# A hybrid decoder step on one core: what the first stage loads and computes, and the order around the output projection

## The chip, the cores and the metric

One Trainium2 chip, one core. The metric is the device time of one execution in microseconds. One core has TensorE (PE in the profile, its weight loads PEld), VectorE (DVE), ScalarE (ACT), GpSimd (POOL) and SyncE (SP). SP and ACT each issue transfers on a DMA queue of their own (SPq, ACTq).

## The reference, cut to what matters

A prompt of 512 tokens and 8 sample tokens (520 rows of 1024) pass one layer: adaLN modulation, RMSNorm, an input projection, sparse attention and a gated recurrence, an output projection, and a mixture of experts. What the change touches:

```python
sh_a, sc_a, gt_a, sh_f, sc_f, gt_f = split(silu(c) @ w_ada + b_ada, 6)
h = rms_norm(x, g_pre_mix) * (1.0 + sc_a) + sh_a
q, kv_c, kv_s, kv_w, gates, hq, hf, hi, hog = split_projection(h @ w_in)
kvc = compress_kv(concat([pool_c[page_table], kv_c]), w_phi1, b_phi1, w_phi2)   # samples: 8 x 1024 cached rows
mixed = concat([rms_norm(o_nsa), o_hgrn]) @ w_out
x = x + gt_a * rms_norm(mixed)
```

`compress_kv` turns each chunk of cached rows into one row by two small matmuls with a gelu between them. The modulation weights `w_ada` are 1024 x 6144, in three parts of 1024 x 2048 (8.4 MB each): part 0 (shift and scale before the mixer) is needed before the input projection, parts 1 and 2 only after the output projection.

## The kernel before, in words

The program is written with generators. `play(order, ...)` advances one generator per letter of a string, which sets the program order. A planner then places each engine's instructions by that order and its own estimate of when inputs are ready and buffers free, so an instruction can come ahead of earlier ones on its engine. `issue_after(i)` holds what a block creates on the engine of instruction `i` behind `i`.

Stage A, played by `ORD_A` (line 56, played at line 373), has three generators:

- `x`, `normed(t)` (line 348), five times: a tile of 128 rows of x is loaded on ACT's queue, squared and summed, scaled, and transposed on TensorE into `xnT`.
- `a`, `ada(0)` (line 218): for each of 8 values of k two tiles of 128 x 1024 of `w_ada` (512 KB each) are loaded on SP's queue into the buffers `mh0` to `mh3` and `wa`, and multiplied with `sT`. At the end the bias and gain table `bg` (512 KB) goes into the next of the same buffers (line 235), and VectorE makes `mod0` (lines 237, 240).
- `s`, `sample_compress` (line 296): the 8 samples' cached pages are loaded in 8 batches `cg` of 8 pages (128 KB a page, 1 MB a batch, three batches buffered), first stage 32 matmuls (line 311, into PSUM bank `pf` or `po` in turn), evacuated and passed through the gelu on ScalarE and VectorE (lines 318 to 322, 275 to 279), second stage 8 matmuls (lines 326 and 329). One batch is two letters.

After stage A: the first projection's weights `wr0` (512 KB) are loaded into buffer `mh1` and split in a high and a low part (lines 374 to 377, helper lines 114 and 115), `mod0` is transposed (line 380), and `hhi`, `hlo` (the modulated rows in two parts) are made (lines 382 to 393).

Stage B, played by `ORD_B` (line 539): ten projections of 48 matmuls and a narrow one for the gates (`n`, lines 410 and 474), the rest of `samples`, and parts 1 and 2 of the modulation (`a`) with 1 MB loads into two buffers, whose memory is free only when `hlo` is done. The result goes to DRAM (`MOD`). Parts 1 and 2 accumulate in `pf`. The stages that follow (recurrence, attention) are bound by the same engine.

Output projection: the last attention block `attn(3)` (`d`, line 1060) has eight steps of scores (lines 1071, 1073), exponentials (line 1077) and values (line 1085). `ORD_E` (line 60, played at line 1230) plays it with the splits of the first half of `w_out` (`f`, line 1211: `ewh` and its low part) and of `mixT` (`mhh`). `wout` (line 1294) is the projection, `wout_samples` (line 1307) the one for the samples, `router_weights` (line 1363) transposes a table of the modulation for the router.

Of the kernel before, what the change touches and what calls it, by code (L numbers as in the profile page):

```python
# [11 lines left out]
F32 = mybir.dt.float32  # L12
# [38 lines left out]
NWA = 1  # L51
FIRST = 6
# [3 lines left out]
ORD_A = "xaxsaaxaxssssaaaxsassaaas"  # L56
ORD_B = "ssnaasnaanaanaanaasnaanaansnaannsnassnasaa"
# [9 lines left out]
def body(tc, I, O):  # L67
# [45 lines left out]
    def split(src, hi, lo, eng=None):  # L113
        act.activation(hi, src, AF.Copy)  # L114
        (eng or dve).tensor_tensor(lo, src, hi.bitcast(F32), op=ALU.subtract)  # L115

# [101 lines left out]
    def ada(gq, tiles, ps_1, mod):  # L218
        p = ps_1()
        for k in range(KT):  # L220
            if gq:
                w2 = tiles()
                sp.dma_start(w2, I["wa"][gq, k].rearrange("j p n -> p j n"))
            for j in range(2):
                if gq:
                    wa = w2[:, j]
                else:
                    wa = tiles()
                    sp.dma_start(wa, I["wa"][gq, k, j])
                for q in range(2):  # L230
                    r = slice(64 * j + 32 * q, 64 * j + 32 * q + 32)
                    pe.matmul(p[r, :], sT[:, k, :], wa[:, 512 * q:512 * q + 512], start=(k == 0), stop=(k == KT - 1))
            yield
        bg = (tiles()[:, 0] if gq else tiles()).rearrange("p (a b) -> p a b", a=2)
        sp.dma_start(bg, I["bg"][gq])
# [52 lines left out]
    sp.dma_start(w1c, I["wphi"])  # L288
    w2c = pc_.tile([64, 2, 64], F32, name="w2c")
    sp.dma_start(w2c, I["wphi2"])  # L290
    b1c = pc_.tile([64, 2], F32, name="b1c")
    sp.dma_start(b1c, I["b1"])
# [3 lines left out]
    def sample_compress():  # L296
        cgs = []
# [6 lines left out]
        for b in range(8):  # L304
# [3 lines left out]
            p = (ps_f if b % 2 and b < FIRST else ps_o)()  # L308
# [57 lines left out]
    def all_normed():  # L366
        for t in range(5):
            normed(t)
            yield

    was = itertools.cycle([lambda c=c: mslot[c](F32, D) for c in range(4)] + [lambda: p0.tile([128, D], F32, name="wa", bufs=1)] * NWA)
    samples = sample_compress()
    play(ORD_A, x=all_normed(), a=ada(0, lambda: next(was)(), lambda: ps_mm()[:, 0], mod0), s=steps(samples, ORD_A.count("s")))
    wr0 = mslot[1](F32, KT, 128)
    act.dma_start(wr0, I["wi"][0])
    wi0 = [mslot[c](F32R, KT, 128) for c in (2, 3)]
    split(wr0, *wi0)
# [157 lines left out]
    def modulations():  # L535
        for gq in (1, 2):
            yield from ada(gq, lambda: wap.tile([128, 2, D], F32, name="wa", bufs=2), ps_f, None)
# [650 lines left out]
    with contextlib.ExitStack() as order:  # L1188
# [21 lines left out]

        def wout_half(hf, wh, wl):
# [18 lines left out]
        play(ORD_E, h=hs, d=gens["d"], f=fh)  # L1230
# [62 lines left out]

    def wout(hf, t, wh, wl):
        pm = ps_mm()
        for kk in (2, 3, 0, 1):
            for k2 in range(2):
                k = 2 * (kk % 2) + k2
                a, b = (mhi[k], mlo[k]) if kk < 2 else (mhh[k], mlh[k])
                for j, (a, b) in enumerate(((a, wh), (a, wl), (b, wh))):  # L1300
                    pe.matmul(pm[:, kk // 2], a[:, 128 * t:128 * t + 128], b[kk][:, k2],
                              start=(k == 0 and j == 0), stop=(k == 3 and j == 2))
        m = x1[t][:, 512 * hf:512 * hf + 512]
# [59 lines left out]
    def router_weights():  # L1363
        dve.tensor_tensor(cW[:, 0], router(GC.rearrange("p a b -> p (a b)"), 128, wrt), brt, op=ALU.add)
# [690 lines left out]
```

## Time and profile before

| | us |
|---|---|
| median of 3 runs | 747.39 (746.75 to 752.22) |
| profiled execution | 741.32 |
| its span | 739.6 |
| mean granted clock of TensorE | 0.958 of full |

The span is the part of the profiled execution in which engines work; 1.7 us lie around it. "Idle before" in a row is the time its engine stood still ahead of it and, after the arrow, what ended that. In a window's row the numbers are busy microseconds, with the count of instructions in brackets.

### The profile page before, as it was taken

To read this page: it belongs to the slowest core of one execution; us is meant where nothing else is said; L and a number is where in the kernel's file an instruction comes from. 1 tells how busy PE (TensorE), PEld (TensorE's weight loads), DVE (VectorE), ACT (ScalarE), POOL (GpSimd) and SP (SyncE) were. 2 spreads that over 40 slices of the span, in tenths; PEclk is the share of its full clock that TensorE was granted. 3 is DMA by queue.
4 is the path that set the end of the run, shared out by engine and by line. 5 is a ranking of instruction groups with operands and counts; after the bars stand their busy time and mean duration, and the time that the engine had idled before them with its cause. 6 is when DMAs were issued, how large, how long until landed. Compare 5 with 4: busy or idle time off the path is not lost. (4 is left out here: it accounts for less than half of the span.)

```text
span 739.6 us, 13131 instructions
## 1 busy us (share of the span) xinstructions
PE 643.4 (87%) x4510; PEld 480.1 (65%) x4510; DVE 456.3 (62%) x1092; ACT 372.2 (50%) x770; POOL 153.4 (21%) x183
## 2 busy tenths in 40 slices
PE   3886898999899989899999989995889999999940
PEld 1754766779688778799776546573456677666620
DVE  3722623345686875667885254456887966888824
ACT  3322523324554545462554545346475757888833
POOL 1000310001141050150110131634211222222113
PEclk9998999999999999999999999998799999999985
DMA  8887698875554545312632274349899889998526
GB/s 282 278 292 252 219 322 294 309 260 176 184 181 143 174 125 182 118 58 85 265 119 84 92 250 140 120 136 345 279 384 356 260 230 321 346 331 287 156 31 231
DMA packets 74605, 160.83 MB, mean 217 GB/s; under 512 B 11346, under 2 KB 39538, under 8 KB 74146
## 3 DMA queue, kind: packets, MB, share of 16 engines
q1 hardware_dynamic: 59808, 125.98, 49.7%
q10 hardware_dynamic: 10690, 25.39, 10.1%
q0 software_dynamic: 4032, 8.53, 5.3%
q8 instruction: 38, 0.62, 0.4%
q14 instruction: 37, 0.30, 0.1%
HBM read 145.29 MB, written 24.28 MB: 229 GB/s over the span
## 5 line engine op out<-in xcount | busy, mean ns | idle before, releaser
L576 PE MATMUL pp<-hhi,wh 128*128 128x260 f32 x256 | 74.9, 292 | 0.3 <-ACT kvt L454 0.3
L576 PE MATMUL pp<-hlo,wh 128*128 128x260 f32 x256 | 73.1, 286 | 0.0
L576 PE MATMUL pp<-hhi,wl 128*128 128x260 f32 x256 | 72.9, 285 | 0.0
L1720 POOL DMA_INDIRECT Y<-ot,gi x17 | 24.4, 1438 | 129.9 <-ACT ot L1719 122.8
L668 ACT ACTIVATE jn<-P,M 128x128 bf16<-128x128 f32 (+3 forms) x64 | 35.9, 561 | 29.2 <-DVE M L666 24.0
L576 PEld LDWEIGHTS pp<-hhi,wh 128*128 128x128 f32 x256 | 48.2, 188 | 3.1 <-issue 2.4
L576 PEld LDWEIGHTS pp<-hlo,wh 128*128 128x128 f32 x256 | 48.2, 188 | 2.0 <-issue 1.8
L576 PEld LDWEIGHTS pp<-hhi,wl 128*128 128x128 f32 x256 | 48.2, 188 | 1.4 <-issue 1.2
L115 DVE TENSOR_TENSOR wl<-wr,wh 128x1024 fp32r<-128x1024 f32 x9 | 11.3, 1250 | 38.4 <-ACT wh L114 38.4
L1077 ACT ACTIVATE PT<-mm 128x256 f32<-128x256 f32 x80 | 24.3, 389 | 19.8 <-PE mm L1073 19.8
L666 DVE CUSTOM_DVE_ANT_0 P<-mm,tb 128x128 f32<-128x128 f32 (+3 forms) x64 | 29.1, 484 | 5.8 <-PE mm L659 5.8
L410 PE MATMUL mm<-hhi,wh 128*128 128x260 f32 x144 | 30.0, 288 | 1.3 <-ACT wh L114 1.3
L114 ACT ACTIVATE wh<-wr 128x1024 fp32r<-128x1024 f32 x9 | 9.5, 1056 | 41.7 <-PE mm L410 22.1
L410 PE MATMUL mm<-hlo,wh 128*128 128x260 f32 x144 | 30.0, 285 | 0.0
L659 PE MATMUL mm<-ka,qs 128*128 128x512 f32 (+2 forms) x112 | 27.3, 352 | 3.1 <-DVE mx L779 1.7
L1691 PE MATMUL pf<-ewi,xh 128*96 128x512 f32 x72 | 29.8, 413 | 0.0
L410 PE MATMUL mm<-hhi,wl 128*128 128x260 f32 x144 | 29.8, 287 | 0.0
L1691 PE MATMUL pf<-ewi,xl 128*96 128x512 f32 x72 | 28.8, 400 | 0.0
L1718 ACT ACTIVATE ot<-mm 96x512 f32<-96x512 f32 x17 | 10.1, 594 | 33.3 <-PE mm L1715 33.3
L1073 PE MATMUL mm<-qs,ka 128*128 128x512 f32 x80 | 25.6, 399 | 0.0
L410 PEld LDWEIGHTS mm<-hhi,wh 128*128 128x128 f32 x144 | 22.2, 188 | 5.0 <-issue 3.4
L410 PEld LDWEIGHTS mm<-hhi,wl 128*128 128x128 f32 x144 | 22.2, 188 | 3.5 <-issue 3.4
(657 smaller groups left out, 1838.6 us busy)
## 6 DMA issues: line engine op xcount, KB each, us to landing
ewr<-in_ew SPq DMA_DIRECT2D x37, 512.0 KB
wa<-in_wa SPq DMA_DIRECT2D x16, 1024.0 KB
wr<-in_wi ACTq DMA_DIRECT2D x25, 512.0 KB
ewt<-in_ew SPq DMA_DIRECT2D x24, 512.0 KB
cg<-in_cc SPq DMA_DIRECT2D x64, 128.0 KB
ewh<-in_ew SPq DMA_DIRECT2D x16, 512.0 KB
x<-in_ew SPq DMA_DIRECT2D x15, 512.0 KB
mh<-in_wa SPq DMA_DIRECT2D x13, 512.0 KB
```

The source lines that it names most:

```text
L114: act.activation(hi, src, AF.Copy)
L115: (eng or dve).tensor_tensor(lo, src, hi.bitcast(F32), op=ALU.subtract)
L410: pe.matmul(p[:, hf, 0:260], a[:, k, :], b[:, k, hf * 260:hf * 260 + 260], start=(k == 0 and j == 0), stop=(k == KT - 1 and j == 2))
L576: pe.matmul(p[:, 0:260], a[:, k, :], b[:, k, c], start=(k == 0 and j == 0), stop=(k == KT - 1 and j == 2))
L659: pe.matmul(o, QS[g][:, h % 4, qc], KA[g][:, j, a:b], start=(j == 0), stop=(j == 1))
L666: dve.tensor_tensor_reduce(out=p, in0=sb[:, br], in1=tb0[:, 384 - 128 * i:512].rearrange("p (k n) -> p k n", n=128), scale=SL[h], scalar=1 ...
L668: act.activation(jn[:, 0:128 * (i + 1)], p.rearrange("p k n -> p (k n)"), AF.Exp, scale=-1.0, bias=M[:, 0, i, br, h:h + 1], accum_out=M[:, ...
L1073: pe.matmul(S[:, br], KS[g][:, q, br, j], QS[g][:, :, qc], start=False, stop=(q == 1))
L1077: act.activation(PT[:, :, h], S4[:, :, h], AF.Exp, scale=-SL[4 * g + h])
L1691: pe.matmul(pg, a[:, k, :], b[:, wk_], start=(k == 0 and j == 0), stop=(k == 7 and j == 2))
L1718: act.activation(o3[:, 0], pd[:, 0], AF.Copy)
L1720: pool.indirect_dma_start(out=Y, out_offset=bass.IndirectOffsetOnAxis(ap=gix, axis=0), in_=ot, in_offset=None, bounds_check=T - 1, oob_is_ ...
```

## The change

- Stage A plays only `x` and `a` (`ORD_A`). The `w_ada` tiles are now 1 MB (both halves of one k), in four buffers: two tiles in the memory of `AK` and `AG`, two in that of `qs0` and `qs1`. `bg` has a tile of its own, loaded on ACT's queue after the last x tile, as is `wr0`, which is also split there.
- The loads of `w_phi1`, `w_phi2`, `b_phi1` and all of `sample_compress` belong to stage B (`ORD_B`), every batch in PSUM bank `po`.
- Parts 1 and 2 of the modulation use four 1 MB buffers: `AK`, `AG` and the two of before.
- `split` returns its ScalarE instruction. In `ORD_E` the steps of `attn(3)` after the first are held on ScalarE behind the second split of `w_out` (one step) or the fourth (the others). The first transposes of `router_weights` are held on TensorE behind the first `wout`.

```diff
-ORD_A = "xaxsaaxaxssssaaaxsassaaas"
-ORD_B = "ssnaasnaanaanaanaasnaanaansnaannsnassnasaa"
+ORD_A = "xaxaxaxaxaaaa"
+ORD_B = "nsasnasansasnasansasnasansasnasansasnasansanaa"
...
     def split(src, hi, lo, eng=None):
-        act.activation(hi, src, AF.Copy)
+        cut = act.activation(hi, src, AF.Copy).ins
         (eng or dve).tensor_tensor(lo, src, hi.bitcast(F32), op=ALU.subtract)
+        return cut
...
+            w2 = tiles()
+            sp.dma_start(w2, I["wa"][gq, k].rearrange("j p n -> p j n"))
             for j in range(2):
-                if gq:
-                    wa = w2[:, j]
-                else:
-                    wa = tiles()
-                    sp.dma_start(wa, I["wa"][gq, k, j])
+                wa = w2[:, j]
...
     def sample_compress():
+        sp.dma_start(w1c, I["wphi"])
+        sp.dma_start(w2c, I["wphi2"])
+        sp.dma_start(b1c, I["b1"])
...
-            p = (ps_f if b % 2 and b < FIRST else ps_o)()
+            p = ps_o()
...
-        for t in range(5):
+        for t in range(4):
             normed(t)
             yield
+        normed(4)
+        act.dma_start(wr0, I["wi"][0])
+        act.dma_start(bg0, I["bg"][0])
+        split(wr0, *wi0)
+        yield
...
+    two = [lambda n=n: wide(at1.tile([128, 2 * D], F32, name=n)) for n in ("AK", "AG")]
+    was = itertools.cycle(two + [lambda n=n: wide(nso.tile([128, 2 * D], F32, name=n)) for n in ("qs0", "qs1")])
...
+        was = itertools.cycle(two + [lambda: wap.tile([128, 2, D], F32, name="wa", bufs=2)] * 2)
         for gq in (1, 2):
-            yield from ada(gq, lambda: wap.tile([128, 2, D], F32, name="wa", bufs=2), ps_f, None)
+            yield from ada(gq, lambda: next(was)(), ps_f, None)
...
-                split(raw[c], high[c], lo, en(93 + c))
+                cuts.append(split(raw[c], high[c], lo, en(93 + c)))
...
-        play(ORD_E, h=hs, d=gens["d"], f=fh)
+        last = dict(h=hs, d=gens["d"], f=fh)
+        for n, c in enumerate(ORD_E):
+            with tc.issue_after(cuts[1 if n < 6 else 3]) if cuts and c == "d" else nullcontext():
+                next(last[c], None)
+        play("", **last)
...
+        wout_end.append(mm.ins)
...
-        dve.tensor_tensor(cW[:, 0], router(GC.rearrange("p a b -> p (a b)"), 128, wrt), brt, op=ALU.add)
+        with tc.issue_after(wout_end[0]):
+            dve.tensor_tensor(cW[:, 0], router(GC.rearrange("p a b -> p (a b)"), 128, wrt), brt, op=ALU.add)
```

## Rows read from the trace of the kernel before

**Rows 1.** Part 1 of the page: busy time, share, instructions.

```profile
PE 643.4 (87%) x4510; PEld 480.1 (65%) x4510; DVE 456.3 (62%) x1092; ACT 372.2 (50%) x770; POOL 153.4 (21%) x183
```

**Rows 2.** Windows: busy by engine, granted clock, DMA share, GB/s.

```profile
core 0: us, PE busy (x) PEld busy (x) DVE busy (x) ACT busy (x) POOL busy (x), PEclk, DMA share, GB/s
0.00:76.17 76.17, 51.45 (x342) 36.07 (x342) 30.18 (x112) 23.53 (x55) 2.82 (x20) 0.93 0.81 269
64.00:70.00 6.00, 2.79 (x15) 2.53 (x16) 1.38 (x2) 0.00 (x0) 0.00 (x0) 0.76 0.90 291
76.17:183.00 106.83, 99.38 (x806) 79.65 (x806) 45.08 (x81) 36.43 (x66) 13.43 (x19) 1.00 0.79 269
0.00:5.00 5.00, 0.00 (x0) 0.00 (x0) 0.00 (x0) 1.59 (x2) 2.23 (x15) 1.00 0.55 182
5.00:10.00 5.00, 0.00 (x0) 0.00 (x0) 0.00 (x0) 0.40 (x2) 0.00 (x0) 1.00 1.00 370
35.00:40.00 5.00, 3.90 (x32) 2.62 (x30) 0.70 (x2) 0.91 (x3) 0.00 (x0) 1.00 0.93 337
```

**Rows 3.** Lines of TensorE, 0 to 76.17 us.

```profile
L311 PE MATMUL po<-cg,w1c 128*128 128x128 f32 x98 | 14.6, 305 | 0.8 <-DMA cg<-in_cc 0.8
L311 PE MATMUL pf<-cg,w1c 128*128 128x128 f32 x96 | 14.0, 307 | 2.7 <-DMA cg<-in_cc 2.7
```

**Rows 4.** Timeline of the SP queue: start us, us, line, transfer.

```profile
63.53 0.38 SPq L235 DMA_DIRECT2D mh<-in_bg  x1
...
79.27 0.33 SPq L215 DMA_DIRECT2D mh<-in_csk  x1
```

**Rows 5.** Timeline of TensorE: start us, us, line [idle before].

```profile
62.72 1.05 PE L232 MATMUL mm<-mh,sT 128*32 128x512 f32 x4 [1.56 <-DMA mh<-in_wa]
...
76.17 0.51 PE L410 MATMUL mm<-hhi,mh 128*128 128x260 f32 x2 [0.87 <-ACT mh L114]
...
90.73 0.33 PE L326 MATMUL pt<-hidc,w2c 64*64 64x64 f32 x4
```

**Rows 6.** Timeline of VectorE and ScalarE, 57 to 73 us.

```profile
57.48 0.27 ACT L318 ACTIVATE Bsc<-po 64x128 f32<-64x128 f32 x1 [2.51 <-PE po L311]
...
60.89 0.42 DVE L279 SCALAR_TENSOR_TENSOR hidc<-huc,hidc 64x256 f32<-64x256 f32 x1 [0.48 <-ACT huc L278]
...
68.43 0.69 DVE L237 TENSOR_TENSOR mod<-mm,mh 128x512 f32<-128x512 f32 x1 [7.12 <-DMA mh<-in_bg]
...
72.00 0.80 ACT L391 ACTIVATE hhi<-xnT,modT 128x512 fp32r<-128x512 f32 x1
```

**Rows 7.** Timeline of TensorE, one whole batch of compression.

```profile
172.94 3.73 PE L311 MATMUL po<-cg,w1c 128*128 128x128 f32 x32
176.43 0.49 PE L410 MATMUL mm<-hhi,wh 128*128 128x260 f32 x2
```

**Rows 8.** Waits of TensorE, 76 to 168 us: total, times, longest.

```profile
PE pf L232 <- DMA wa<-in_wa: 5.1, 8, 1.5
```

**Rows 9.** Timeline of ScalarE before the output projection.

```profile
424.30 3.89 ACT L114 ACTIVATE ewh<-wq 128x1024 fp32r<-128x1024 f32 x4
428.09 1.66 ACT L114 ACTIVATE mhh<-mixT 128x512 fp32r<-128x512 f32 x3
429.65 2.01 ACT L1077 ACTIVATE PT<-mm 128x256 f32<-128x256 f32 x7
```

**Rows 10.** Timeline of TensorE at the same place.

```profile
426.02 0.63 PE L1073 MATMUL mm<-qs,ka 128*128 128x512 f32 x2
429.11 1.92 PE L1314 MATMUL pf<-ewr,msn 128*32 128x512 f32 x2 [2.46 <-DVE ewr L115]
...
432.55 0.65 PE L1085 MATMUL po<-PT,VT 128*64 128x256 f32 x4
```

**Rows 11.** Waits of ScalarE, 395 to 470 us.

```profile
ACT PT L1077 <- PE mm L1073: 13.5, 8, 3.3
```

**Rows 12.** Timeline of TensorE, the router's first transposes.

```profile
444.70 1.09 PE L1347 MATMUL pt<-ident,tab 128*128 128x128 f32 x8
```

More of the change, by code (lines that the diff above doesn't have):

```diff
@@ L3 @@
 import contextlib
-from contextlib import ExitStack
+from contextlib import ExitStack, nullcontext
 import numpy as np
@@ L50 @@
 LOP = ()
-NWA = 1
-FIRST = 6
 DMAN = False
 NCG = 3
-ORD_A = "xaxsaaxaxssssaaaxsassaaas"
-ORD_B = "ssnaasnaanaanaanaasnaanaansnaannsnassnasaa"
+ORD_A = "xaxaxaxaxaaaa"
+ORD_B = "nsasnasansasnasansasnasansasnasansasnasansanaa"
 ORD_C = "PPPrPsPrPPrPsPrPPsPrPPrPsPrPPrsPPPrPsPrPPrttsPPrPPrsPPPrsPPrPPrsPPrPsPPrPPrsPPrttPsPrPPrPsPPrPsPrPPrPsPrPPsPrPPrPsPrttPPrsPPrPPsPrPPrsPPrPPrsPPPrsPPPPsPPPsPPPPPPPPPtt"
@@ L215, in paged, with ada @@
                 sp.dma_start(t[:, p], I[src][bass.ds(rs[p], 1)].rearrange("o p f -> p (o f)"))
-    def ada(gq, tiles, ps_1, mod):
+    def ada(gq, tiles, ps_1, mod, bg=None):
         p = ps_1()
         for k in range(KT):
-            if gq:
-                w2 = tiles()
-                sp.dma_start(w2, I["wa"][gq, k].rearrange("j p n -> p j n"))
+            w2 = tiles()
+            sp.dma_start(w2, I["wa"][gq, k].rearrange("j p n -> p j n"))
             for j in range(2):
-                if gq:
-                    wa = w2[:, j]
-                else:
-                    wa = tiles()
-                    sp.dma_start(wa, I["wa"][gq, k, j])
+                wa = w2[:, j]
                 for q in range(2):
@@ L233, in ada @@
             yield
-        bg = (tiles()[:, 0] if gq else tiles()).rearrange("p (a b) -> p a b", a=2)
-        sp.dma_start(bg, I["bg"][gq])
+        if bg is None:
+            bg = tiles()[:, 0].rearrange("p (a b) -> p a b", a=2)
+            sp.dma_start(bg, I["bg"][gq])
         mod = bg[:, 0] if mod is None else mod
@@ L287, in body @@
     w1c = pc_.tile([128, 2, 8, 128], F32, name="w1c")
-    sp.dma_start(w1c, I["wphi"])
     w2c = pc_.tile([64, 2, 64], F32, name="w2c")
-    sp.dma_start(w2c, I["wphi2"])
     b1c = pc_.tile([64, 2], F32, name="b1c")
-    sp.dma_start(b1c, I["b1"])
     cw = open_pool("cw", 1, s_cw)
@@ L366, in all_normed, with wide @@
     def all_normed():
-        for t in range(5):
+        for t in range(4):
             normed(t)
             yield
-    was = itertools.cycle([lambda c=c: mslot[c](F32, D) for c in range(4)] + [lambda: p0.tile([128, D], F32, name="wa", bufs=1)] * NWA)
-    samples = sample_compress()
[L373 to L377, printed above, removed]
+        normed(4)
[3 more added lines that the diff above has]
+        yield
+    bg0 = p0.tile([128, 2, 512], F32, name="bg0")
+    wr0 = mslot[1](F32, KT, 128)
+    wi0 = [mslot[c](F32R, KT, 128) for c in (2, 3)]
+    def wide(t):
+        return t.rearrange("p (j n) -> p j n", j=2)
+    two = [lambda n=n: wide(at1.tile([128, 2 * D], F32, name=n)) for n in ("AK", "AG")]
+    was = itertools.cycle(two + [lambda n=n: wide(nso.tile([128, 2 * D], F32, name=n)) for n in ("qs0", "qs1")])
+    samples = sample_compress()
+    play(ORD_A, x=all_normed(), a=ada(0, lambda: next(was)(), lambda: ps_mm()[:, 0], mod0, bg0), s=steps(samples, ORD_A.count("s")))
     pt = ps_t()
@@ L1209, in halves @@
             return x.rearrange("p (a b) -> p a b", a=2)
+        cuts = []
         def wout_half(hf, wh, wl):
@@ L1292, in body @@
     rn = aft.tile([128, 4], F32, name="rn")
+    wout_end = []
     def wout(hf, t, wh, wl):
@@ L1300, in wout @@
                 for j, (a, b) in enumerate(((a, wh), (a, wl), (b, wh))):
-                    pe.matmul(pm[:, kk // 2], a[:, 128 * t:128 * t + 128], b[kk][:, k2],
+                    mm = pe.matmul(pm[:, kk // 2], a[:, 128 * t:128 * t + 128], b[kk][:, k2],
                               start=(k == 0 and j == 0), stop=(k == 3 and j == 2))
+        wout_end.append(mm.ins)
         m = x1[t][:, 512 * hf:512 * hf + 512]
```

## The prediction, made before the changed kernel ran

> **What bounds the kernel now.** I read the page's engine shares first. TensorE is busy 87% of the span, the next engine 62% [rows 1], so a gain has to come from a stretch in which TensorE stands still or does work that could be done elsewhere in time. I then cut the front of the span into windows [rows 2]. Up to 76.17 us, where the first matmul of the input projection starts, TensorE is busy 51.45 of 76.17 us while transfers are busy 0.81. From there to 183 us, where the projections end, it is busy 99.38 of 106.83. So the first stretch is bound by loads and the second by TensorE. In the first stretch TensorE's idle time is 24.7 us, and much of what keeps it busy is compression: 98 and 96 of its 256 first-stage matmuls run there [rows 3], so 194 in all. Compression isn't needed by the first projection; it shares the SP queue with the weights that are. The reader should see two things at the end of the stretch. The table `bg` is issued at 63.53 [rows 4], when the last modulation weights are already being multiplied (62.72 [rows 5]), and VectorE can start on it only at 68.43, after 7.12 us of idle time [rows 6]. And the first projection waits for the split of `wr0` (the releaser in its row, [rows 5]), although the first modulated rows are ready at 72.00 + 0.80 = 72.80 [rows 6].
>
> **Stage A after the change.** Before the projections can start, these must land: 16 x 512 KB of `w_ada` (8.39 MB), x (2.13), `bg` and `wr0` (0.52 each), `cT` and small tables (about 0.25): 11.8 MB by the shapes in the code. The pages and the 1 MB of `w_phi1` are no longer among them. The rate: two windows with full queues show 370 and 337 GB/s, mean 354; the first 5 us moved only 182 x 5 = 0.91 MB, what full rate moves in 2.6 us, so the start costs 2.4 us [rows 2]. 2.4 + 11.8/0.354 = 35.7 us for the last weights. Four 1 MB buffers in flight hold 11 us of transfer, and a buffer is freed by eight small matmuls, so I take the queue as never empty. Behind the last tile: eight matmuls, 2 x 1.05 = 2.1 us [rows 5]; then the chain from VectorE's addition to the first modulated rows, 72.80 - 68.43 = 4.4 us [rows 6], now without the wait for `bg`; 0.2 us of hand-over is an estimate from the gaps between those rows. First projection: 35.7 + 2.1 + 4.4 + 0.2 = 42.4 instead of 76.17, so 33.8 us earlier. The bounds: at 370 GB/s throughout it is 41, and at the 269 of the whole stretch now [rows 2] it is 53. I take the full-queue rows, since SP now has four whole tiles to queue; the low end stays for the range.
>
> **What stage B takes over.** 194 first-stage matmuls: a whole batch of 32 delays the next matmul from 172.94 to 176.43, so 3.49 us [rows 7], and 194/32 x 3.49 = 21.2 us. Five second stages came before 76.17; the first four matmuls of one take 0.33 us [rows 5] and the other four I put at as much, so 5 x 0.66 = 3.3 us. Together 24.5 us, all on the engine that bounds stage B: nothing hides it. Its ScalarE and VectorE parts (the chain of rows 6, from 57.48 to 61.31, is 3.8 us a batch with its waits) lie beside projections: VectorE is busy 45 and ScalarE 36 of 107 us there [rows 2].
>
> TensorE's idle time in stage B is 106.83 - 99.38 = 7.4 us, of which 5.1 are waits for `wa` [rows 2, 8]. Four buffers instead of two take some of that away, about half by my choice (2.5); the page loads now share the queue, and I put the same 2.5 against it. Bounds: 5 us gained if all waits for `wa` go; 12 lost if they treble. The rate asked for: 269 GB/s over both stretches [rows 2] is 49.2 MB in 183 us; less the 11.8 of stage A it is 37 MB from 42 to 174 us, 283 GB/s, under the 337 to 370 that full queues give. So I take the middle, zero. SP, too, has more queued behind each wait: a page load that waits for its batch's buffer holds back `wa` loads and the `kvT` stores behind it, and TensorE waits for the former; that is in the bound of 12.
>
> The single PSUM bank `po` makes each batch's first stage wait for the evacuation of the one before. It costs nothing while projection matmuls stand between; if not, up to 3.8 us a batch [rows 6]. I take zero, since stage B has 48 projection matmuls for each letter `n`. The early split of `wr0` and the table of its own are in the 42.4. `AK` and `AG` are now written by VectorE only after the last modulation load in them is used; `MOD` is stored well before that stage, so nothing, at most the few us of one store. Stages A and B together: 33.8 - 24.5 + 0 = 9.3 us. The stages behind are bound by TensorE as well, so a shift passes through.
>
> The row on the clock: in the stretch 64 to 70 us, where TensorE was busy 2.79 of 6 us, the granted clock was 0.76, a mixture of the levels 2.4 and 1.2 GHz; over 76 to 183 it was 1.00 [rows 2]. The Trainium skill, "TensorE: Matmul & The Clock Gate", section "Part 1: The HAM clock gate", says that the lower clock is the default and only sustained activity releases it, which speaks against emptying stage A. By that rule stage B would begin slow, at up to 6 x 0.24 = 1.4 us. By the row the kernel pays this already at the same place, so the sum gets no term.
>
> **Output projection.** ScalarE does four splits of `w_out` and three of `mixT` (424.30 to 429.65) ahead of seven exponentials of the last attention steps [rows 9]. TensorE ends its scores at 426.02 + 0.63 = 426.65, idles, does four small matmuls of the samples and reaches the values at 432.55 [rows 10]: 5.9 us for little work. With the splits held ahead of the second and third step they fall where ScalarE now waits for scores (13.5 us over eight waits [rows 11]). Four splits cost 3.9 us, of which I let 2 show, since two come in a row ahead of each of two steps. With 0.4 us of useful matmuls: 5.9 - 0.4 - 2 = 3.5 us gained. Bounds: 5.5, if all hide; -2, if the splits only move and hold TensorE earlier, with their whole 3.9 us. The hold on the router: its transposes come at 444.70 [rows 12], already behind the first `wout` in the order now, so zero, either way.
>
> **Sum.** 9.3 + 3.5 = 12.8 us. The profiled execution took 741.3 (span 739.6 and 1.7 around it), so its like would take 728.5. That execution lies 6.1 us under the median of 747.4; I assume the same distance, so 734.6 for the median.
>
> **Rivals.**
> 1. *The stage isn't loaded alone.* The planner may move pages up into SP's gaps, so that the old interleaving returns. For it: a page load of a later stage (`mh` from `csk`) is issued at 79.27, ahead of stage B's weights [rows 4]. Against it: with four tiles in flight SP has few gaps, and that one came alone. Then what stays is the early `bg` (68.43 less 62.72 + 1.05, the end of the last weights' matmuls, = 4.7) and `wr0` (76.17 - 72.80 = 3.4), less 1.05/0.354 = 3.0 for both tables within the loads that bind, and the 3.5 of the output projection: 747.4 - 8.6 = 738.8. The Trainium skill, "DMA: Bandwidth & Descriptors", section "Queues, rings and completion order", says that descriptors of one ring are consumed in order; by it pages issued behind the last weights couldn't delay them. No row here shows it.
> 2. *Stage B waits for transfers.* Pages and weights queue behind each other on SP and TensorE's waits grow by 10 us. For it: 5.1 us of waits already [rows 8]. Against: the rate above. 734.6 + 10 = 744.6, no change.
> 3. *Slower: the gelu chain is uncovered.* In order, on one PSUM bank, TensorE stands the 3.8 us of rows 6 at each of the 8 batches: 8 x 3.8 = 30 us, 734.6 + 30 = 764.6. For it: all batches share `po`, and the letters often put only an `a` between the two stages of a batch. Against: ample projection matmuls, which the planner can place between. It decides against the change from 20.3/8 = 2.5 us a batch on (then 1% slower).
>
> **How the numbers follow.** A measurement of this kernel can tell about 1%, 7.5 us. Chances: forecast 0.62 (its own range 727 to 742), rival 1 0.15, rival 2 0.16, rival 3 0.07. Faster by over 1% (under 739.9): 0.57 of the forecast, 0.09 of rival 1, 0.02 of rival 2, 0.68. Slower by over 1%: rival 3, 0.07. Within 1%: 0.25. For the range I leave out rival 3 and the ends: 724 (full rate and all waits gone) to 748 (rival 2 with the output projection gaining nothing).
>
> **What would show it.** Right: the first projection matmul between 40 and 46 us; no compression matmul before it; no long wait of VectorE for `bg`; TensorE idle under 10 us from there to the projections' end, at about 174; the splits of `w_out` between the first steps of the last attention block, and values following scores at the end within 3 us. Wrong: compression matmuls ahead of the first projection (rival 1); waits for `cg` or `wa` over 10 us (rival 2); waits of second stages for `hidc` or of first stages for `po` (rival 3); a first projection after 50.

## The result, and the profile after

The changed kernel takes 768.1 us (median of 4 runs, 765.1 to 771.7), the kernel before took 748.3 in the runs beside it: ratio 1.027, interval 1.022 to 1.031. It is slower by about 20 us, and 20 us above the range of the prediction. The profiled execution took 771.66.

The page of the changed kernel, its head and its line of engine shares:

```profile
span 769.9 us, 13131 instructions
PE 666.2 (87%) x4510; PEld 489.8 (64%) x4510; DVE 456.6 (59%) x1092; ACT 374.3 (49%) x772; POOL 150.4 (20%) x183
```

TensorE has as many instructions as before and is busy for 22.8 us more [rows 1]. So most of the loss isn't idle time. Up to the end of the projections the times came out near the forecast. Windows of the changed kernel (to the first projection, to the first matmul of the recurrence's projections, to the last of these, and four shorter stretches):

```profile
core 0: us, PE busy (x) PEld busy (x) DVE busy (x) ACT busy (x) POOL busy (x), PEclk, DMA share, GB/s
0.00:43.22 43.22, 19.77 (x109) 7.57 (x109) 19.61 (x73) 13.95 (x25) 2.22 (x15) 0.92 0.89 334
43.22:174.60 131.38, 126.12 (x1040) 106.47 (x1040) 58.45 (x121) 47.04 (x100) 17.91 (x45) 0.97 0.76 261
174.60:365.60 191.00, 178.18 (x1328) 142.25 (x1329) 116.64 (x417) 83.67 (x213) 30.58 (x45) 0.94 0.38 115
43.22:47.00 3.78, 3.27 (x11) 2.68 (x12) 3.75 (x7) 3.78 (x7) 1.52 (x2) 0.50 0.81 257
47.00:51.00 4.00, 4.00 (x23) 4.00 (x23) 3.96 (x7) 1.25 (x2) 2.37 (x2) 0.59 0.00 1
160.00:173.30 13.30, 13.30 (x113) 11.29 (x113) 7.91 (x12) 3.00 (x7) 3.86 (x22) 1.00 0.48 140
318.00:330.00 12.00, 7.14 (x101) 4.31 (x101) 0.68 (x1) 3.58 (x8) 2.26 (x11) 0.58 0.81 260
```

The same stage of the kernel before, between the first and the last matmul of line 576 (581 after the change):

```profile
183.20:345.40 162.20, 153.22 (x1328) 132.51 (x1329) 117.20 (x418) 81.73 (x213) 37.95 (x66) 1.00 0.43 135
```

TensorE's timeline of the changed kernel, around the first projection, and two rows of VectorE's:

```profile
34.68 1.07 PE L226 MATMUL mm<-qs,sT 128*32 128x512 f32 x8
40.60 1.08 PE L384 MATMUL pt<-ident,mod 128*128 128x128 f32 x4 [4.86 <-DVE mod L235]
43.22 0.80 PE L414 MATMUL mm<-hhi,mh 128*128 128x260 f32 x2 [1.53 <-ACT hhi L395]
...
36.75 0.36 DVE L113 TENSOR_TENSOR wgl<-wgr,wgh 128x192 fp32r<-128x192 f32 x1 [2.78 <-ACT wgh L112]
39.04 0.69 DVE L232 TENSOR_TENSOR mod<-mm,bg 128x512 f32<-128x512 f32 x1
```

The first projection starts at 43.22 instead of 76.17 [rows 5], and the recurrence's projections at 174.6 instead of 183.2, 8.6 us earlier. They hold the same 1328 matmul records as before, but take 191.0 us instead of 162.2: TensorE is busy 25.0 us longer in them and idle 3.8 us longer. Here the gain is lost more than three times over. Beside these projections the stage holds the attention of the eight samples, in two rounds of four: scores against pages of keys `csk` (line 826, after the change 831), scores against a window (830, 835), values from pages `csv` (868, 873). The pages go into the four buffers `mh`, in the order keys, values, keys, values. Lines of TensorE in this stage, of the changed kernel:

```profile
L831 PE MATMUL pt<-mh,qb 128*32 128x512 f32 x32 | 15.5, 604 | 0.0
L873 PE MATMUL po<-mh,PTs 128*32 128x128 f32 x128 | 10.5, 351 | 4.4 <-DMA mh<-in_csv 4.3
L835 PE MATMUL pt<-wnp,qb 128*32 128x512 f32 x16 | 7.3, 605 | 0.0
```

and of the kernel before:

```profile
L826 PE MATMUL pt<-mh,qb 128*32 128x512 f32 x32 | 5.9, 600 | 0.0
L868 PE MATMUL po<-mh,PTs 128*32 128x128 f32 x128 | 7.4, 283 | 0.0
L830 PE MATMUL pt<-wnp,qb 128*32 128x512 f32 x16 | 4.2, 603 | 0.0
```

The mean of one record of a score matmul is the same, 600 and 604 ns; the time in which any of them runs rose from 5.9 to 15.5 us. Before, several ran at once. In the timeline of the changed kernel one score matmul (two records) stands alone among projections:

```profile
205.47 0.28 PE L581 MATMUL pp<-hlo,wh 128*128 128x260 f32 x1
205.58 0.28 PE L581 MATMUL pp<-hhi,wl 128*128 128x260 f32 x1
205.80 1.05 PE L831 MATMUL pt<-mh,qb 128*32 128x512 f32 x2
206.78 0.39 PE L581 MATMUL pp<-hhi,wh 128*128 128x260 f32 x1
```

and in that of the kernel before seven stand in a row:

```profile
201.28 1.49 PE L826 MATMUL pt<-mh,qb 128*32 128x512 f32 x11
202.18 0.59 PE L830 MATMUL pt<-wnp,qb 128*32 128x512 f32 x1
202.59 0.61 PE L826 MATMUL pt<-mh,qb 128*32 128x512 f32 x3
```

Projections start 0.11 to 0.13 us apart; around the lone score matmul 1.20 us lie between two of them (205.58 to 206.78), so it costs 1.08 us. The seven of before and a window score among them took 201.28 to 203.20, 0.24 us for each of the eight. In that row the records start in groups of up to four, 0.43 to 0.45 us apart, while the two records of the lone matmul, 0.45 us apart, have such places to themselves. The Trainium skill, "TensorEngine Tiling (Array Packing)", section "Key Properties", says that matmuls on different tiles of the array can run in parallel, with which these rows agree. It also says that a change of the tiling mode drains TensorE; no run here shows that by itself.

Beside the new order stand later pages on the SP queue. Page loads of the changed kernel (start, length of the group, count):

```profile
173.26 27.55 SPq L214 DMA_DIRECT2D mh<-in_csk  x32
203.54 11.32 SPq L214 DMA_DIRECT2D mh<-in_csv  x8
...
247.49 26.94 SPq L214 DMA_DIRECT2D mh<-in_csk  x32
...
318.53 4.46 SPq L214 DMA_DIRECT2D mh<-in_csv  x8
```

and the keys of the first round in the kernel before, besides the one at 79.27 [rows 4]:

```profile
112.65 1.41 SPq L215 DMA_DIRECT2D mh<-in_csk  x3
124.21 1.90 SPq L215 DMA_DIRECT2D mh<-in_csk  x4
167.30 14.38 SPq L215 DMA_DIRECT2D mh<-in_csk  x22
185.51 1.31 SPq L215 DMA_DIRECT2D mh<-in_csk  x2
```

Before, the last key page was issued at 186.8, ahead of the first score at 199.8. Now the pages are issued from 173.26 to 200.8, while the first score stands at 188.0: the stage that uses them begins earlier, the pages come later. The score matmuls start on TensorE at these times (us; a row by the starts of its first and its last record), in the first and the second round:

```
before: 199.84, seven 201.28 to 202.60 | 254.47, seven 256.37 to 257.69
after:  187.99, three 189.43 to 190.74, 194.21, 197.32, 202.58, 205.80 |
        254.13, 256.60, 261.02, 264.20, 269.89, 272.97, 278.66, 281.75
```

At the end of the stage the values of the second round wait for pages, and too little other work is left. TensorE's timeline of the changed kernel:

```profile
317.37 0.27 PE L704 MATMUL pt<-ident,c 128*48 128x128 f32 x1 [1.56 <-DVE c L697]
...
320.64 2.04 PE L873 MATMUL po<-mh,PTs 128*32 128x128 f32 x24 [2.15 <-DMA mh<-in_csv]
324.80 2.13 PE L873 MATMUL po<-mh,PTs 128*32 128x128 f32 x33 [2.12 <-DMA mh<-in_csv]
```

Over 318 to 330 us TensorE is busy 7.14 of 12, the granted clock is 0.58, a mixture of 2.4 and 1.2 GHz. Over the whole stage the mean of a value matmul rose from 283 to 351 ns.

Most of the rest of the loss is in the last attention block: from its first to its last score (line 1073, 1078 after) 82.0 us instead of 73.8. ScalarE's timeline of the changed kernel:

```profile
426.84 1.28 ACT L1040 ACTIVATE hq<-hq,rql 128x128 f32<-128x128 f32 x4
432.60 0.34 ACTq L1150 DMA_DIRECT2D out_sh<-S  x1
433.53 0.31 ACT L1165 ACTIVATE sq<-osn 128x128 f32<-128x128 f32 x1 [5.41 <-DVE osn L1159]
...
434.40 3.88 ACT L112 ACTIVATE ewh<-wq 128x1024 fp32r<-128x1024 f32 x4
438.18 1.18 ACT L1082 ACTIVATE PT<-mm 128x256 f32<-128x256 f32 x4
```

The splits of `w_out` lie behind ScalarE's wait for the samples' rows `osn` (5.41 us), and by the hold all further exponentials lie behind the splits. So nothing fills that wait; before, exponentials stood on both sides of it, and the splits came ahead of the last seven [rows 9]. TensorE waits with it; its waits in this block, of the changed kernel, are 6.0 us (0.6 before):

```profile
PE pf L1329 <- DVE ewr L113: 4.1, 1, 4.1
PE pt L1170 <- DVE osn L1167: 1.9, 1, 1.9
```

### The profile page after: what moved, and what is told of

It reads as the page before. It is cut to its first block, busy times and chain, and to the rows that moved or that the text cites. A ratio compares the mean times of both kernels' runs of the same rounds, so it can differ in the third digit from the quotient of the medians.

```text
span 769.9 us, 13131 instructions
## 1 busy us (share of the span) xinstructions
PE 666.2 (87%) x4510; PEld 489.8 (64%) x4510; DVE 456.6 (59%) x1092; ACT 374.3 (49%) x772; POOL 150.4 (20%) x183
## 3 DMA queue, kind: packets, MB, share of 16 engines
q10 hardware_dynamic: 10834, 25.92, 10.2%
## 5 line engine op out<-in xcount | busy, mean ns | idle before, releaser
L581 PE MATMUL pp<-hlo,wh 128*128 128x260 f32 x256 | 75.4, 295 | 0.0
L581 PE MATMUL pp<-hhi,wl 128*128 128x260 f32 x256 | 74.8, 292 | 0.0
L581 PEld LDWEIGHTS pp<-hhi,wh 128*128 128x128 f32 x256 | 49.9, 195 | 6.8 <-issue 5.4
L581 PEld LDWEIGHTS pp<-hlo,wh 128*128 128x128 f32 x256 | 49.9, 195 | 3.8 <-issue 3.6
L581 PEld LDWEIGHTS pp<-hhi,wl 128*128 128x128 f32 x256 | 49.9, 195 | 2.4 <-issue 2.3
L1736 POOL DMA_INDIRECT Y<-ot,gi x17 | 24.4, 1437 | 129.4 <-ACT ot L1735 114.9
L306 PE MATMUL po<-cg,w1c 128*128 128x128 f32 x256 | 31.8, 277 | 0.2 <-issue 0.2
L306 PEld LDWEIGHTS po<-cg,w1c 128*128 128x128 f32 x256 | 29.9, 192 | 2.3 <-issue 2.0
L1078 PE MATMUL mm<-qs,ka 128*128 128x512 f32 x80 | 25.8, 399 | 0.0
```

The lines of the kernel that those rows point to most:

```text
L306: pe.matmul(p[:, 128 * k:128 * k + 128], w1c[:, k, s, :], cg[:, :, k, s, :], start=(s == 0), stop=(s == 7))
L581: pe.matmul(p[:, 0:260], a[:, k, :], b[:, k, c], start=(k == 0 and j == 0), stop=(k == KT - 1 and j == 2))
L1078: pe.matmul(S[:, br], KS[g][:, q, br, j], QS[g][:, :, qc], start=False, stop=(q == 1))
L1736: pool.indirect_dma_start(out=Y, out_offset=bass.IndirectOffsetOnAxis(ap=gix, axis=0), in_=ot, in_offset=None, bounds_check=T - 1, oob_is_ ...
```

## The experiments

The table holds every kernel, in us. "Stage" is the recurrence's projections from the first to the last start of their matmuls, "attention" the prompt's last blocks from the first to the last start of their scores, "way behind" from there to the last start of the first output projections, all from the profiled execution, with starts read to 0.1 us; "median" and "ratio" are timed, with the 95% interval. The ratio is to runs of the kernel before made beside each (medians 746.8 to 748.7). Between stage and attention lie 7.0 to 7.1 us in each kernel, and behind the way 25.8 to 27.0 to the first matmul of the experts, but where the text says otherwise.

| kernel | first projection | stage starts | stage | attention | way behind | median | ratio |
|---|---|---|---|---|---|---|---|
| before | 76.2 | 183.2 | 162.2 | 73.8 | 78.1 | 748.3 | |
| changed | 43.2 | 174.6 | 191.0 | 82.0 | 79.3 | 768.1 | 1.027 (1.022 to 1.031) |
| e1_no_holds | 43.0 | 172.4 | 187.4 | 72.8 | 90.0 | 771.7 | 1.033 (1.025 to 1.041) |
| e2_only_holds | 77.2 | 185.9 | 168.3 | 82.7 | 72.5 | 754.7 | 1.010 (1.006 to 1.014) |
| e3_pages_early | 43.2 | 181.9 | 178.7 | 83.0 | 77.2 | 763.6 | 1.020 (1.013 to 1.028) |
| e4_scores_grouped | 43.1 | 174.2 | 174.8 | 81.7 | 80.0 | 757.6 | 1.013 (1.006 to 1.021) |
| e5_router_hold_only | 43.1 | 175.9 | 190.7 | 72.9 | 87.1 | 771.5 | 1.031 (1.022 to 1.039) |
| e6_grouped_no_step_hold | 43.0 | 173.6 | 177.9 | 72.8 | 86.1 | 754.4 | 1.007 (1.003 to 1.011) |
| e7_before_pages_late | 78.3 | 181.7 | 165.0 | 73.9 | 78.1 | 746.0 | 0.997 (0.993 to 1.001) |
| e8_issues_behind_splits | 43.1 | 173.8 | 169.0 | 73.0 | 84.5 | 752.7 | 1.005 (1.002 to 1.008) |
| e14_late_step_hold | 43.1 | 173.8 | 171.4 | 72.9 | 85.0 | 749.1 | 1.000 (0.996 to 1.003) |
| e15_letters_of_before | 67.7 | 181.3 | 166.4 | 84.5 | 78.7 | 756.1 | 1.010 (1.006 to 1.014) |
| e16_letters_and_tail | 70.6 | 180.0 | 166.6 | 72.6 | 83.4 | 748.3 | 0.998 (0.994 to 1.003) |
| e17_late_zero | 43.1 | 176.5 | 174.4 | 72.9 | 85.2 | 756.6 | 1.014 (1.009 to 1.019) |
| e18_changed_late_zero | 43.1 | 173.7 | 191.7 | 83.1 | 77.4 | 775.9 | 1.040 (1.034 to 1.047) |
| e19_before_late_zero | 76.9 | 181.4 | 167.3 | 73.9 | 82.3 | 755.2 | 1.013 (1.008 to 1.018) |
| e20_letters_tail_zero | 70.8 | 184.7 | 163.5 | 73.1 | 87.5 | 754.2 | 1.010 (1.006 to 1.014) |
| e21_hold_two_steps | 43.2 | 174.3 | 173.9 | 72.9 | 82.9 | 747.7 | 1.001 (0.998 to 1.003) |

One execution's stage is known to some 4 us either way only: e2_only_holds has TensorE's order of before up to the last attention block, and its stage took 168.3 us where before it took 162.2, at a granted clock of 0.96 against 1.00; e6, e8, e14, e17 and e21 share another order and took 169.0 to 177.9, mean 173.3. The changed kernel, e1, e5 and e18 share one order there as well: 187.4 to 191.7, mean 190.2. Before, e2 and e19: 162.2 to 168.3, mean 165.9. So the stage costs about 24 us more by the change, by these means.

**e1, e2, e5: which hold costs what.** e1 takes both holds out of the changed kernel, e5 only that of the attention steps, e2 puts both into the kernel before.

```diff
# e1 and e5 (e2 is the reverse, on the kernel before)
-        for n, c in enumerate(ORD_E):
-            with tc.issue_after(cuts[1 if n < 6 else 3]) if cuts and c == "d" else nullcontext():
-                next(last[c], None)
+        for c in ORD_E:
+            next(last[c], None)
# e1 alone
-        with tc.issue_after(wout_end[0]):
+        with nullcontext():
             dve.tensor_tensor(cW[:, 0], router(GC.rearrange("p a b -> p (a b)"), 128, wrt), brt, op=ALU.add)
```

> The changed kernel without its two holds at the output projection; loading order, buffers and letters stay. From the end of the stage of the hgrn projections to the last matmul of the first output projections the changed kernel took 168.2 us, the kernel before 158.8. Theory H (the holds cost these 9.4 us): 768.1 - 9.4 = about 759. Theory S (the loss comes from the sample attention, whose pages now start late on SP; the holds are neutral): 765 to 771. The prediction's own term (the holds gain 3.5): about 771.6.

> The kernel before with only the two holds of the change. Theory H: 748.3 + 9.4 = about 758. Theory S: 745 to 751, since nothing of the loading order is touched. The prediction's own term: 748.3 - 3.5 = about 745.

> The changed kernel with the hold on the router kept and the hold of the last attention steps behind the splits taken away. With both holds the score matmuls of the prompt's attention took 82.0 us from first to last and the way from there to the end of the first output projections 79.3; with neither 72.8 and 90.0 (there TensorE stood before the router's transposes); in the kernel before 73.8 and 78.1. Theory H2 (the hold of the steps costs attention 9 us, the hold of the router saves what the run with neither lost behind it): about 73 and 79, so 768.1 - 9 = about 759. Rival (the splits need the hold, they come late without it): attention 73, but 88 to 90 behind it, and 766 to 772.

Theories H and H2 failed as put. The hold of the steps does cost attention 9 us, in either kernel (82.0 and 82.7 with it, 72.8 to 73.8 without), but without it the changed kernel gives the 9 us back behind: 87.1 and 90.0 instead of 79.3. The rival of e5 is right. In e2, too, theory S missed (745 to 751), and so did the prediction's own term (about 745). In e5 TensorE waits there for a split (its waits):

```profile
PE mm L1314 <- ACT mhh L112: 10.6, 1, 10.6
```

ScalarE has the splits at 457.4, behind seven loads of tables that it issues from 449.55. On the kernel before, both holds together cost 8 us (interval 5 to 11 by the ratio), of which 3.3 are in the two columns (155.2 against 151.9). In the changed order no cost of them in the time can be seen: e1, without both, took 771.7, and e5, without that of the steps, 771.5.

**e3, e4: the pages or the order.** e3 asks for the first round's key pages during the projections (its text says that the kernel before has ten of them there; by the rows above it has eight); e4 moves no load, but issues each group of four score matmuls behind the one that needs the last page.

```diff
# e3: four letters k in ORD_B; the loads of the first round leave sample_attention
+    def first_pages():
+        for bb in range(4):
+            t_ = mslot[bb](F32, 8, 128)
+            paged(t_, 8 * bb, 8, "csk")
+            early.append(t_)
+            yield
# e4
-                for bb in range(4):
+                last = None
+                for bb in (3, 0, 1, 2):
+                    with tc.issue_after(last) if last else nullcontext():
+                        mm = pe.matmul(S[32 * bb:32 * bb + 32, :], qb[:, 4 * r + bb, :], SLK[bb][:, 4 * q:4 * q + 4, :], start=True, stop=True)
+                    last = last or mm.ins
```

> The changed kernel with the 32 page loads of the first four samples' keys put among the loads of the projections (one group of eight at four places of the order), as the kernel before has ten of them; everything else stays. Theory S: the stage of the hgrn projections takes about 162 us again instead of 191, so 768.1 - 29 = about 739, the score matmuls stand four in a row again and their busy time falls from 15.5 to about 6 us. Rival B (the transfers of the projections' stage leave no room, early pages only hold TensorE there): the first hgrn projection moves from 174.6 to 180 or later, and the time is 755 to 768.

> The changed kernel with only the order of the sample attention's score matmuls held: each group of four is issued behind the one that needs the last page, so that four stand in a row on TensorE; no load is moved. If the loss lies in the lone matmuls themselves: their busy time falls from 15.5 to about 6 us and the time by about 9, to 759. If it lies in the pages' lateness (the chain scores, values, next pages ends 33 us later while TensorE has little left beside it): busy time falls as well, the stage still ends at 360 or later, and the time is 762 to 770.

e4 did what the theory of the lone matmuls said: a line, the window of its stage, and its wait for pages of values:

```profile
L833 PE MATMUL pt<-mh,qb 128*32 128x512 f32 x32 | 4.3, 605 | 0.0
...
174.20:349.00 174.80, 163.15 (x1329) 137.46 (x1329) 117.33 (x417) 83.92 (x213) 31.56 (x45) 0.95 0.41 126
...
PE po L876 <- DMA mh<-in_csv: 4.1, 2, 2.9
```

The scores' busy time fell from 15.5 to 4.3 us, TensorE's busy time in the stage from 178.2 to 163.2, and the time is 10.5 us lower. The wait for pages of values, 4.3 us in the changed kernel, stays; behind it the granted clock is 0.82 over 290 to 310 us and 0.75 over 310 to 330. In e3 the scores stood in rows too (busy 4.9 us), but of the 29 us expected only 5 came. Its rival B holds beside it: the weights of the modulation now come behind the pages, and TensorE waits for them at the end of the projections. Its waits, and the window in which they lie:

```profile
PE pf L226 <- DMA wa<-in_wa: 7.5, 2, 6.0
...
169.60:181.90 12.30, 5.05 (x27) 0.66 (x25) 3.29 (x4) 3.57 (x11) 0.50 (x2) 0.76 0.75 259
```

With its scores in rows and no wait for pages of values its stage still takes 178.7 us; it begins behind these waits at a granted clock of 0.69 (181.95 to 200 us).

**e7: late pages by themselves.** The kernel before, its first round's key pages held behind the last store of the modulation (`stored[1]`).

```diff
-                paged(t_, 8 * b, 8, "csk")
+                with nullcontext() if r else tc.issue_after(stored[1]):
+                    paged(t_, 8 * b, 8, "csk")
```

> The kernel before with the page loads of the first four samples' keys all issued behind the last store of the modulation, as the changed kernel issues them; here the score matmuls still stand four in a row on TensorE. Theory S in its first form (late pages by themselves cost the stage): the stage of the hgrn projections grows from 162 to 175 us or more and the time to 760 or more. Theory O (the order of TensorE costs, the pages' lateness only makes that order): under 755, the stage 162 to 169 us.

Theory O: no loss can be measured. The last of these pages was issued at 195.2 instead of 186.8, and still the scores stand in a row. So lateness of that size in the first round costs nothing by itself. Of the second round e7 tells nothing: its last eight pages of values are issued from 283.7 us on, in the kernel before from 284.0, but in e4 from 300.8 and in the changed kernel from 318.5. In each kernel with the new letters but e3 TensorE waits 3.6 to 4.7 us for such pages in the stage, and in none with the letters of before.

**e6, e8, e14, e21: repairs at the end of attention.** On e4's base: e6 groups the window scores as well and drops the hold of the steps; e8 issues ScalarE's seven table loads (`tab`, `row`, `wrt`, `brt`, `sel20`) behind the eight splits; e14 and e21 hold the last four and the last eight exponentials behind the four splits of `w_out`.

```diff
# e8
+        with tc.issue_after(cuts[7]):
+            act.dma_start(tab, m4[g, j, :, 8, :].unsqueeze(0).to_broadcast([128, 2, 512]))
...
# e14 (n >= 18), e21 (n >= 16)
+            with tc.issue_after(cuts[3]) if n >= 18 and c == "d" else nullcontext():
                 next(last[c], None)
```

> The changed kernel with the score matmuls of the samples grouped as in e4_scores_grouped, the window scores grouped in the same way, and the hold of the last attention steps taken away, the router's kept. If the two losses are separate and add: 757.6 - 9 for the steps - 3 for the window scores (their busy time was 7.9 us against 4.2 in the kernel before) = about 746, level with the kernel before. If the loss of the sample attention is the pages' lateness in the end: the stage of the hgrn projections stays at 175 us and only the steps' 9 us come back, 749. If the holds give nothing: 757.

> e6_grouped_no_step_hold with ScalarE's seven loads of the router's and modulation's tables issued behind the eight splits at the end of attention, instead of ahead of them. In e6_grouped_no_step_hold TensorE waited 10.5 us for the split of mixT there, and the way from the last score to the end of the first output projections took 86.1 us (78.1 in the kernel before). Theory (ScalarE's issues, 8 us from 449.5 to 457.4 in e5_router_hold_only, hold the splits): the way shrinks to about 79 and the time from 754.4 to about 747. Rival (the router's rows come late in exchange, and TensorE waits there): 752 to 757.

> e8_issues_behind_splits with the last four exponentials of attention held behind the four splits of w_out, where the kernel before has seven of them; so the splits lie between attention steps, but behind ScalarE's wait for the sample rows and not the other way round. Theory (the change's hold costs because it takes the filling work out of that wait): attention takes 73 to 76 us from first to last score, not 82, and the way behind it about 74 to 78; 743 to 747. Rival (any hold of steps costs what it gains): attention 78 or more, and the time is within 3 of e8_issues_behind_splits.

> e14_late_step_hold with the last eight exponentials of attention behind the four splits instead of the last four (seven in the kernel before). Theory (what decides the end of attention is how many exponentials stand behind the splits: with all of them attention grows by 9 us, with four or none TensorE starts the output projection before its splits are there and the way behind grows by 7, with seven or eight neither happens): attention 73 to 75 and the way behind it 77 to 79, together about 152 as in the kernel before, and about 749.1 - 6 = 743. Rival (the number does not matter, the sum is 156 to 158 whatever stands behind the splits in the changed order): 747 to 751.

e6 gained 3 us on e4, not 12: the two losses are not separate terms. e8 shortened the way behind by 1.6 us of the 7 expected (its time lies in the rival's range), e14 and e21 left it at 85.0 and 82.9, where theory had 79 at most. Attention and the way behind together take 151.9 us before, 161.3 in the changed kernel and 155.8 to 158.9 in these four: 2.4 to 5.5 us of the 9.4 lost at this place come back, and no place of the splits that was tried brings all of it, as the rival of e21 says. e21 is level with the kernel before.

**e15, e16: the letters of before.** The changed kernel, and e14, with `ORD_A` and `ORD_B` of before, so that the samples are compressed beside the first loads again; tables, tiles and buffers stay.

```diff
-ORD_A = "xaxaxaxaxaaaa"
-ORD_B = "nsasnasansasnasansasnasansasnasansasnasansanaa"
+ORD_A = "xaxsaaxaxssssaaaxsassaaas"
+ORD_B = "ssnaasnaanaanaanaasnaanaansnaannsnassnasaa"
```

> The changed kernel with the letters of the first two stages as in the kernel before, so that the samples are compressed beside the loading of the first modulation again; the early table, the early first rows, the wider tiles, the four buffers and the holds stay. Theory O (the sum of the transfers before the samples' pages is the same in either order, so an earlier first projection brings the sample attention no earlier; with the letters of before its score matmuls stand in a row): first projection at 60 to 72 us, the stage of the hgrn projections 162 to 170 us long and the time 748 to 755, the rest above the kernel before being the holds. Rival (the loss comes from the buffers and tables): stage above 175 us, 762 or more.

> e14_late_step_hold with the letters of the first two stages as in the kernel before. If the two repairs add: the stage of the hgrn projections 162 to 168 us long, attention and the way behind it 148 to 152 us together as in the kernel before (151.9) or better, and the time 738 to 745, level with the kernel before or under it. If the loss of the first stages is still there: 748 or more.

e15 is 12 us faster than the changed kernel though its first projection is 24.5 us later: the stage takes 166.4 us, and its scores stand in rows but for one pair (7.0 us busy). The buffers and tables, which stay in it, are therefore not what makes the stage long. The 8 us by which it is above the kernel before are as much as the holds alone cost in e2; e16, which mends the end as well, is level with the kernel before. Its two repairs don't bring what was expected of them: attention and the way behind it take 156.0 us, not 148 to 152, and the time is not under 745. e16 against e14 is the cleanest measure of the change's main part, since both have their scores grouped and the same end: first projection at 70.6 or 43.1, median 748.3 or 749.1. The 27.5 us make no difference that can be measured (each interval is some 3 us either way): the stage starts 6.2 us later in e16 and is 4.8 us shorter.

**e17 to e20: the zeros.** Behind the attention ScalarE issues five stores of zeros into `Y`; in the changed kernel it then stands still for 14.2 us, of which the five issues take 10.2; before it was 7.7 and 6.0. These runs issue them behind the third evacuation of the output projection, on e14, the changed kernel, the kernel before and e16.

```diff
-    for t in range(5):
-        n = 128 if t < 4 else 8
-        act.dma_start(Y[128 * t:128 * t + n].rearrange("t (a b) -> t a b", a=4), zero[0:n].unsqueeze(1).to_broadcast([n, 4, 256]))
...
+        if len(taken) == 3:
+            with tc.issue_after(out):
+                for i in range(5):
...
```

> e14_late_step_hold with ScalarE's five stores of zeros into Y issued behind the third evacuation of the output projection, no longer ahead of the first. In e14_late_step_hold these stores and the wait behind them held ScalarE from 434.7 to 447.9, the first evacuation came at 453.3 and TensorE waited 3.4 us for it; the way from the last score to the end of the first output projections took 85.0 us. Theory (ScalarE's queue behind the stores is what keeps the end of the attention stage long): way about 78, time about 749.1 - 7 = 742. Rival (the waits for the splits and the low clock behind them hold it): way 83 or more, 747 to 751.

> The changed kernel with only the five stores of zeros moved behind the third evacuation. There ScalarE waited 14.2 us for them (7.7 in the kernel before) and TensorE 4.5 us for the evacuation of the samples' rows. Theory: 79.3 us for the way from the last score to the end of the first output projections shrink to about 74, and the time from 768.1 to about 763; the rest of the loss lies ahead of it. Rival (the stores collide with the loads of w_out wherever they stand): 766 to 770.

> The kernel before with only the five stores of zeros moved behind the third evacuation. TensorE has no wait there for an evacuation over 1 us, so by the theory the way from the last score to the end of the first output projections stays at 76 to 78 us and the time at 745 to 749. If ScalarE's 7.7 us behind the stores cost TensorE in a way that its waits do not show: 741 to 744.

> e16_letters_and_tail with the five stores of zeros moved in the same way. By the theory of e17_late_zero: its way of 83.4 us behind attention shrinks to about 77 and the time from 748.3 to about 742; with e17_late_zero it tells whether loading the first modulation alone is worth anything once the order behind it is repaired: if so, e17_late_zero is the faster of the two by 2 us or more; if the sample attention's pages decide, the two are equal within 2.

The theory falls: each of the four is 6 to 8 us slower than its base. The way behind barely shrinks (79.3 to 77.4 in e18) or grows, and from its end to the first matmul of the experts it is now 29.2 to 31.4 us instead of 25.8 to 27.0; why is not shown. e17 and e20, with the first projection at 43.1 and 70.8, are again 2.4 us apart, with intervals that overlap, and the one with the earlier projection is the slower.

## Why the prediction was wrong, point by point

- **Stage A: right.** First projection 43.22, predicted 42.4, no compression ahead of it (rival 1 fell), and no wait of VectorE for `bg`. Two misses cancel: the loads ran at 408 GB/s over 10 to 30 us, not 354, and the last `w_ada` matmuls began at 34.68; but the chain behind them took 43.22 - 35.75 = 7.5 us, not 4.6. VectorE began its addition only at 39.04, 3.3 us behind these matmuls: ahead of it stood the split of the gates' weights, for which it waited 2.78 us, and small instructions for a table of the recurrence.
- **Stage B: right, but the sum agrees partly by luck.** It took 131.4 us instead of 107.0, 24.4 more where 24.5 were booked. TensorE's busy time grew by 26.7 us (126.12 against 99.4), the cost of the low clock (next point) among it, and its idle time fell by 2.4, for which zero was booked. Transfers held TensorE less than before (2.3 us of waits for weights against 5.1 [rows 8]), so rival 2 fell, and so did rival 3: 0.2 us of idle time ahead of first stages, 1.4 us of waits for `hidc`. Stages A and B gained 8.6 us of the 9.3 (9.3 by the means of the kernels that share an order: 183.5 less 174.2).
- **The clock after stage A: no term, wrongly.** From 43.22 to 47 us the granted clock was 0.50, to 51 us 0.59: 0.50 x 3.78 + 0.41 x 4 = 3.5 us. In the kernel before it was 1.00 over the whole stretch behind the same point [rows 2], so that this was no cost "already paid". The Trainium skill's rule that I weighed ("TensorE: Matmul & The Clock Gate", "Part 1: The HAM clock gate") had the sign right, my estimate of 1.4 was too small.
- **The step that failed: "The stages behind are bound by TensorE as well, so a shift passes through."** TensorE is busy there in an order that was fixed beforehand, and sample attention needs SP's pages. In every kernel but e3 the run of its key loads follows the last store of the modulation by 1.1 us: it begins at 167.3 before (but for eight pages), 173.3 after and 164.5 in e15, wherever the first projection stands. Reordering the front moved TensorE's work and not these pages. What sets this point in the changed kernel is not the transfers alone: over the last 13.3 us ahead of it TensorE is busy throughout and transfers 0.48 (the row from 160 us above), and SP's longest waits from 155 us on are

```profile
SPq L765 <- ACT VCS L326: 5.3, 1, 5.3
SPq L230 <- PE pf L226: 3.0, 1, 3.0
SPq L242 <- DVE AG L240: 2.8, 1, 2.8
```

  So the pages stand on their queue behind transfers that wait for what stage B computes last: the compressed samples, which the change moved there, and the modulation. Asking for them earlier isn't free either (e3: 7.5 us of waits for weights). The work that could begin earlier met pages that came later, and the scores were placed one by one among projections. The stage took about 24 us more. Shown are the part of the order (with the scores grouped the mean of the stage falls from 190.2 to 173.3, and e4 alone gives 10.5 us of the time), that later pages in the first round cost nothing without it (e7), and that the earlier projection is worth nothing that can be measured once the order is mended (e16 against e14). About 7 us of the 24 stay with the scores grouped, beside the waits for pages of values and a lower clock; that part isn't tested by itself. Not shown is how the planner comes to the spread order: pages asked for earlier (e3, e15) bring the rows back, but e7 keeps them with late pages.
- **Output projection: the sign was wrong.** I booked +3.5 on the ground that ScalarE waits for scores over eight steps, where the splits could lie. They fell into one place, behind the wait for `osn`, and the hold took away what filled it: values now follow the last scores at once (454.99 behind 454.44), as foretold, but earlier in the block no score runs from 432.5 to 443.0 us. Attention lost 8.2 us and the way behind 1.2; with the holds alone on the kernel before it was 8.9 lost and 5.6 gained. The hold on the router was booked at zero; the way behind is 90.0 us without it (e1) and 87.1 with it (e5), one execution each, and the times are level (771.7 and 771.5).
- **Rival 3** was near in its time, 764.6, and had nothing of the cause.

By the profiled executions: -8.6 (stages A and B) + 28.8 (the stage behind) + 8.2 + 1.2 (attention and the way behind) + 0.7 (all that follows) = 30.3, the difference of the spans. The medians differ by 20: the profiled execution of before lies 7 us under its median of 748.3, that of the changed kernel 3.6 over its own.

## What to carry to other kernels

An engine that is busy in a later stage doesn't say that the stage can start earlier: follow the transfers of that stage back on their queue, and see whether they start earlier too. If they still stand behind transfers that wait for the same work, the gain can end there. When an order is planned from estimates, read the new order (who stands between whom on the bottleneck), above all for small matmuls that are cheap only in a row; and before holding instructions on an engine, look at which wait those instructions were filling.

## What the runs showed that was not expected

- A matmul of 32 output columns that stands alone among full ones costs TensorE 1.08 us, in a row 0.24, at the same duration of one record (600 to 604 ns). Sixteen of them spread out cost 15.5 us of busy time, grouped 4.3.
- Two executions with the same order on TensorE in a stage (before, e2) differ by 6 us there: busy 153.2 against 159.1 us, granted clock 1.00 against 0.96. In e2 it was 0.92 over 200 to 220 us, where TensorE was busy throughout, behind a stretch (185.9 to 200 us) in which it was busy 10.76 of 14.1 us.
